# Sums of the up weights loaded straight into the operands' places, and more buffer places, in the feed-forward part of a two-stream trunk layer

## The chip, the cores and the metric

The kernel runs on one core of one Trainium2 chip. The metric is device time in microseconds (us) of one execution, the median of several. Five engines matter: TensorE (PE, its weight loads shown as PEld), VectorE (DVE), ScalarE (ACT), GpSimd (POOL) and SyncE (SP), which here issues every DMA.

## The reference

One layer (DEPTH is 1) over 2048 prompt positions and 32 sample positions, model width 1024, all in float32. A mixer (spatial gating and gated DeltaNet, with causal convolution) is followed by a feed-forward part with width 4096:

```python
h = rmsnorm(x, norm_mix_g[l]) * (1 + sc1) + sh1
m, nb, ns, vr = mixer(h, conv_state[l], delta_state[l], w_in[l], ...)
x = x + gt1 * m
h = rmsnorm(x, norm_ffn_g[l]) * (1 + sc2) + sh2
x = x + gt2 * (jnp.square(jax.nn.relu(h @ w_up[l])) @ w_down[l])
...
y = rmsnorm(x, final_norm_g)
```

The change touches the last two lines of the layer: `h @ w_up`, and what is queued around it.

## The kernel before

All work is first written down as operations of a `Program` (L201), with the engine, an estimated cost and the memory that each reads and writes. `schedule` (L237) then plays a list schedule: for each engine it keeps what is ready, ordered by priority and by the TensorE operation that comes due first, and it writes the program out in the order of the planned start times. So every engine, and SP's queue of DMAs, runs a fixed order; on the chip an instruction waits until what it needs is there, and everything behind it on its engine or queue waits too. Whatever changes an operation or a buffer changes the planned order everywhere.

Scratch memory is a set of `NSLOT` slots of 1056 floats per partition (25 of them). `ring` (L463) names places in slots that are used in turn: `new` takes the next place of a ring, and its next user has to wait until the last one is read.

**First half** (to about 1054 us of the profile): gates, projections, spatial gating and DeltaNet (`startup`, `mixers`), on matmuls into `g` banks, with many small matmuls into `L`, `C`, `B` and `M`. Its rings `pk1`, `pk2`, `kq1`, `kq2` and `E` hold tiles loaded for DeltaNet and for the norms.

**Feed-forward part** (`feed_forward`, L1512, from about 1054 us). The 2080 positions run in four blocks b = 0 to 3 of 520 positions, each as two groups of 260. A matmul in float32 is made of three fp32r matmuls: each operand x is split into a high part (ACT copies it to fp32r) and a low part (DVE or POOL subtracts the high part from x); `mm3` (L411) multiplies high by high, high by low and low by high.

The up product of one step s (16 steps of 256 hidden rows) takes a 2 x 2 block of weight pieces against a 2 x 2 block of h tiles and needs 7 products instead of 8, with four of its weight operands being sums of pieces. In block 0, `up_weights` (L1433) loads the four pieces, POOL makes the sums, they are split into high and low parts, and both parts are stored in DRAM tensors `su_d`. In blocks 1 to 3 the sums come back from `su_d`: each half (128x512, 256 KB) is loaded by a DMA into a place of the staging ring `uraw`, and ACT copies it from there into the operand's place (`wh` or `wl`). The three plain pieces are loaded from `w_u` into staging and split as before. The operands' places `uw` are 8 pairs (high, low) used in turn.

The down product has the same form (`ffn_down`, L1677): 16 half steps u, with sums of its weights kept in `sd_d`, loaded through the staging ring `draw` and split by ACT and DVE into `dw`. From the end of block 0 `uraw` and `draw` are one ring of 8 staging places. Up and down steps alternate on TensorE: down u of step q, then up 2q + 2 + u for the next step. `hidden` (L1629) forms relu squared and the sums of hidden tiles: DVE adds, ACT squares, POOL subtracts, ACT and DVE split.

At a change of block, `h2_values` (run from s = 8) has put the 28 combinations of h tiles of the next block into DRAM (`th_d`), and `h2_load` (L1411) loads them through the ring `fe` and splits them into the tiles `BH` and `BL`; these come free only as the last up step of the block is multiplied, so the loading falls beside the last down step. `settle`, `square` and `final` finish the block's result.

Lines that the profile names: L337 is every ACT instruction, L352 every tensor_tensor of DVE or POOL, L357 every scalar_tensor_tensor, L390 every DMA, L398 every matmul. Tiles in slots are named `s`, with a number in the order below; `f` is a PSUM bank of the feed-forward part. The DMA scratch of the program is left at its default.

Of the kernel before, what the change touches and what calls it, by code (L numbers as in the profile page):

```python
# [10 lines left out]
AF = mybir.ActivationFunctionType  # L11
# [5 lines left out]
P = 128  # L17
# [14 lines left out]
G = 260  # L32
# [3 lines left out]
NC_ = 17  # L36
SLOT = 1056
HALF = 528
NSLOT = 25

PE, DVE, ACT, POOL, DMA, NONE = range(6)
TABLES = {AF.Silu: "silu", AF.Gelu_apprx_tanh: "gelu", AF.Exp: "exp", AF.Ln: "ln"}
# [158 lines left out]
class Program:  # L201
# [35 lines left out]
    def schedule(self):  # L237

        ops = self.ops
        due = [i if o.eng == PE and o.prio == GEMM else len(ops) for i, o in enumerate(ops)]  # L240
        for i in reversed(range(len(ops))):
            due[i] = min([due[i]] + [due[j] for j in ops[i].succ])
        key = [(o.prio, due[i] if o.prio >= EVAC else i, i) for i, o in enumerate(ops)]
        free = [0.0] * 6
        port = [0.0] * 6
        wait = [[] for _ in range(6)]
        ready = [([], []) for _ in range(6)]
        table, grid = None, (P, P)
        order = []

        def release(i, t):
            o = ops[i]
            if o.eng == NONE:
                finish(i, t, t)
            else:
                heapq.heappush(wait[o.eng], (t, i))

        def finish(i, start, end):
            o = ops[i]
            o.start = start  # L260
            order.append((start, i))
            for j in o.succ:
                s = ops[j]
                s.ready = max(s.ready, end + o.lat + LATENCY.get((o.eng, s.eng), 0.0))
                s.npred -= 1
                if s.npred == 0:
                    release(j, s.ready)

        for i, o in enumerate(ops):
            if o.npred == 0 and o.start == 0.0 and o.eng != NONE:  # L270
                heapq.heappush(wait[o.eng], (0.0, i))
        for i, o in enumerate(ops):
            if o.npred == 0 and o.eng == NONE and not any(k == i for _, k in order[-1:]):
                finish(i, 0.0, 0.0)
                o.npred = -1

        other = {DVE: POOL, POOL: DVE}
        while True:
            best = None
            for e in range(5):  # L280
                shared = port[other[e]] - PORT if e in other else 0.0
                t = None
                if ready[e][0]:
                    t = free[e]
                elif ready[e][1]:
                    t = max(free[e], shared)
                if wait[e]:
                    at, i = wait[e][0]
                    at = max(free[e], at, shared if ops[i].port else 0.0)
                    t = at if t is None else min(t, at)  # L290
                if t is not None and (best is None or t < best[0]):
                    best = (t, e)
            if best is None:
                break
            t, e = best
            while wait[e] and wait[e][0][0] <= t:
                i = heapq.heappop(wait[e])[1]
                heapq.heappush(ready[e][ops[i].port], key[i])
            shared = port[other[e]] - PORT if e in other else 0.0
            tops = [q for q in (ready[e][0], ready[e][1] if shared <= t else None) if q]  # L300
            if not tops:
                continue
            i = heapq.heappop(min(tops, key=lambda q: q[0]))[-1]
            o = ops[i]
            end = t + o.cost
            if e == PE:
                if o.table and o.table != grid:
                    end += 195 if o.table == (P, P) else 135
                    grid = o.table
            elif o.table and o.table != table:  # L310
                end += 1280
                table = o.table
            free[e] = end
            if o.port:
                port[e] = end
            finish(i, t, end)
        assert len(order) == len(ops), (len(order), len(ops))
        self.span = max(free)
        order.sort()
        return [ops[i] for _, i in order]  # L320


class Kern:
# [211 lines left out]
    def setup(self):  # L535
# [14 lines left out]
        self.nslab, self.sn = 0, None  # L550
        self.slots = [{"m": Mem(SLOT), "t": None} for _ in range(NSLOT)]
        self.bmem = [Mem(512, whole=True) for _ in range(8)]
        self.banks = {"g": [0, 1, 2], "L": [3], "C": [4, 5], "B": [6], "M": [7]}
        self.rings, self.rshape = {}, {}
        for s in range(NSLOT):
            self.era(s, F32)
        rg = self.ring
        hv = lambda *ss: [(s, lo) for s in ss for lo in (0, HALF)]
        rg("pk2", [(0, 0), (1, 0)], (P, 4, 256))
        rg("kq2", hv(2), (P, 2, 256))  # L560
        rg("N", [(3, 288)], (P, 256))
        rg("U", [(3, 544)], (P, 256))
        self.z0 = self.slot(3, 0, (P, 9, 32))
        rg("nb", [(24, 0), (5, 0)], (P, SLOT))
        rg("pk1", [(6, 0)], (P, 3, 256))
        rg("kq1", hv(7), (P, 2, 256))
        rg("vt", [(8, 0), (8, 256)], (P, 256))
        rg("tmp", [(3, 800)], (P, 64))
        rg("jk", [(8, 768)], (P, 128))
# [36 lines left out]
            small(n, s, 17)  # L606
        rg("gt", [(17, pos[0] + 36 * e) for e in range(4)], (P, H, 9))
        rg("Q", hv(18, 19, 20), (P, 512))
        rg("E", hv(21, 22, 23), (P, 512))
        rg("va", [(q, 256 * e) for q in (18, 19, 20) for e in range(4)][:10], (P, 256))  # L610
        rg("raw", hv(18), (P, 516))
        rg("y", hv(19), (P, 512))
# [754 lines left out]

    def ffn_places(self):
        rg = self.ring
        e = [(s, G * e) for s in (6, 7, 16, 22, 23) for e in range(4)]  # L1370
        for tag, n in (("fe", 6), ("fs", 2), ("fx", 1), ("fp", 1), ("fu", 2), ("fv", 1), ("fr", 3), ("fk", 4)):
            rg(tag, e[:n], (P, G))
            e = e[n:]

# [58 lines left out]
    def up_weights(self, b, s):  # L1433

        quad = lambda q: self.i["w_u"][s, q]
        if b == 0:
            a11, a12, a21, a22 = (self.raw(self.uraw, quad(q)) for q in range(4))
            s1, s2 = (self.turn(self.uraw) for _ in range(2))
            self.tt(s1, a21, a22, ALU.add, POOL)
            self.tt(s2, s1, a11, ALU.subtract, POOL)  # L1440
        out = []

        def sum_(i, x):
            if b == 0:
                hl = self.operand(self.uw, x)
                for e in range(2):
                    self.dma(self.su_d[s][i][e], hl[e].f32())
            else:
                hl = self.turn(self.uw)
                for e in range(2):  # L1450
                    self.act(hl[e], self.raw(self.uraw, self.su_d[s][i][e]), AF.Copy)
            out.append(hl)

        plain = lambda q, x: out.append(self.operand(self.uw, x if b == 0 else self.raw(self.uraw, quad(q))))
        if b:
            s1 = s2 = s3 = s4 = a11 = a12 = a22 = None
        plain(0, a11)
        sum_(1, s2)
        sum_(0, s1)
        if b == 0:  # L1460
            s3 = self.turn(self.uraw) if len(self.uraw) > 6 else a11
            self.tt(s3, a11, a21, ALU.subtract, POOL)
        sum_(2, s3)
        if b == 0:
            s4 = s2
            self.tt(s4, a12, s2, ALU.subtract, POOL)
        sum_(3, s4)
        plain(1, a12)
        plain(3, a22)
        return out  # L1470
# [38 lines left out]
    def plain(self, b, q):  # L1509
        return b == 0 or (b, q) == (NB - 1, 7)  # L1510

    def feed_forward(self):  # L1512
# [8 lines left out]
        wv = [[view(k, e) for e in range(2)] for k in range(2)]  # L1521
        self.p.op(NONE, 0.0, fn, [v for w in wv for v in w], [])
        self.uw = [tuple(wv[k][e][:, 512 * j : 512 * j + 512] for e in range(2)) for k in (self.nslab % 2, (self.nslab + 1) % 2) for j in range(4)]
        for s in (3, 4, 5, 8, 9, 10, 11, 17, 18, 19, 20, 24):
            self.era(s, F32R)
        at = lambda n: slice(G * (n // 7), G * (n // 7) + G)
        self.hp = [[(self.BH[n % 7][:, at(n)], self.BL[n % 7][:, at(n)]) for n in range(4 * i, 4 * i + 4)] for i in range(7)]
# [4 lines left out]
        self.rp8, self.rpa, self.rpb = pairs[:16], pairs[10:], pairs[:10]  # L1532
        two = lambda s: [sl(s, 512 * e, (P, 512)) for e in range(2)]
        self.dw = [(x, y) for s, t in ((4, 5), (8, 9), (10, 3)) for x, y in zip(two(s), two(t))]
        self.uraw = two(0) + two(1) + two(2)
        self.draw = [self.raw1[0][:, 512 * e : 512 * e + 512] for e in range(2)] + two(21)
        self.acc = [[sl(12 + m // 2, G * (2 * (m % 2) + g), (P, G)) for g in range(2)] for m in range(KT)]
# [324 lines left out]
```

## Time and profile before

| what | value |
|---|---|
| median of 3 runs | 2437.33 us (2435.55 to 2437.97) |
| span of the profiled execution, first to last instruction (the page gives no other time of it) | 2450.8 us |
| mean granted TensorE clock | 0.989 |
| first feed-forward matmul starts, last one starts | 1054.1 us, 2439.6 us |
| DMA traffic of the whole program | 574.85 MB, mean 235 GB/s |

Busy time is what an engine spent in instructions; matmuls overlap, so TensorE's count of matmuls in a stage says more than its busy share. An idle time is put down to what released the engine last. In the rows of groups, busy time and mean length (ns) of one instruction are followed by the idle time before them.

### The profile page before, as it was taken

The page shows a single profiled execution, that of the slowest core. Times are in us where ns is not written, and L with a number is a line of the kernel's source. Part 1 is how long each engine was busy: PE and PEld are TensorE (multiplying, and loading weights), DVE is VectorE, ACT ScalarE, POOL GpSimd, SP SyncE. Part 2 cuts the span into 40 slices and gives each one's busy share as a digit, 9 for nine tenths or more (in the row PEclk, how much of TensorE's full clock was granted, in tenths as well). Part 3 has the DMA queues.
Part 4 walks back from the last instruction along what each step waited for, and adds up shares of the span by engine and source line. Part 5 has one row for each costly group of instructions (what it writes and reads, how often), then busy time and mean ns, then how long its engine had stood idle before and what let it go on. Part 6 is the DMA issues. An engine that isn't in the chain of part 4 may idle for free.

```text
span 2450.8 us, 53625 instructions
## 1 busy us (share of the span) xinstructions
PE 2372.3 (97%) x18786; PEld 2217.0 (90%) x18786; DVE 1749.2 (71%) x4041; ACT 1563.5 (64%) x3727; POOL 790.0 (32%) x1079
## 2 busy tenths in 40 slices
PE   7998999999999999999999999999899999899998
PEld 4876878999999878999999999999899999899998
DVE  5555666556665546488677778889788888877786
ACT  4454656455565435375455687777788877887774
POOL 2134422202432223455333453333721213511111
PEclk9999999999999899999999999999999999999999
DMA  8688667555457767888667787888788877787773
GB/s 305 206 298 264 211 199 243 143 180 161 145 181 215 239 183 231 269 273 275 240 215 244 251 265 242 268 273 275 240 266 289 267 256 231 248 279 220 246 232 117
DMA packets 389687, 574.85 MB, mean 235 GB/s; under 512 B 71628, under 2 KB 201568, under 8 KB 389416
## 3 DMA queue, kind: packets, MB, share of 16 engines
q1 hardware_dynamic: 389416, 571.42, 72.2%
q8 instruction: 148, 2.42, 0.4%
q14 instruction: 123, 1.01, 0.1%
HBM read 434.80 MB, written 136.45 MB: 233 GB/s over the span
## 4 chain that ended last, share of the span: by engine, by line
PE 27%; DVE 9%; DMA 8%; ACT 5%; issue 2%; POOL 1%; SPq 0%; DVEq 0%; ACTq 0%; POOLq 0%
PE f L398 27%; DVE s L352 6%; DMA s<-su_d 3%; ACT s L337 2%; DVE s L357 1%; ACT wh L337 1%; DMA s<-w_u 1%; DMA wr<-su_d 1%; DVE wl L352 1%; DVE BL L352 1%; ACT wl L337 1%; DMA wr<-w_u 1%; POOL s L352 1%; DMA s<-sd_d 1%; DMA s<-th_d 0%
## 5 line engine op out<-in xcount | busy, mean ns | idle before, releaser
L337 ACT ACTIVATE s<-s 128x260 f32<-128x260 f32 (+11 forms) x1398 | 611.5, 464 | 338.8 <-DVE s L357 99.5
L398 PE MATMUL f<-s,s 128*128 128x260 f32 x3984 | 538.5, 284 | 8.2 <-ACT s L337 3.6
L352 POOL TENSOR_TENSOR s<-s,s 128x260 f32<-128x260 f32 (+3 forms) x369 | 374.3, 1027 | 518.1 <-ACT s L337 377.0
L398 PE MATMUL f<-BH,wh 128*128 128x260 f32 x1800 | 514.0, 286 | 13.4 <-DVE s L352 9.1
L398 PE MATMUL f<-BH,wl 128*128 128x260 f32 x1800 | 511.1, 284 | 3.6 <-DVE wl L352 2.6
L398 PEld LDWEIGHTS f<-s,s 128*128 128x128 f32 x3984 | 501.8, 189 | 13.6 <-DVE s L352 6.3
L398 PE MATMUL f<-BL,wh 128*128 128x260 f32 x1800 | 509.9, 283 | 1.9 <-DVE BL L352 1.9
L352 DVE TENSOR_TENSOR s<-s,s 128x260 fp32r<-128x260 f32 (+5 forms) x740 | 413.4, 576 | 71.3 <-ACT s L337 43.6
L398 PE MATMUL g<-BH,wh 128*128 128x512 f32 (+2 forms) x1112 | 424.7, 382 | 0.0
L352 DVE TENSOR_TENSOR s<-f,s 128x260 f32<-128x260 f32 x856 | 345.6, 420 | 94.6 <-PE f L398 91.4
L398 PE MATMUL g<-BH,wl 128*128 128x512 f32 (+2 forms) x1112 | 395.0, 355 | 0.0
L398 PE MATMUL g<-BL,wh 128*128 128x512 f32 (+2 forms) x1112 | 393.8, 354 | 0.6 <-DVE BL L352 0.6
L398 PEld LDWEIGHTS f<-BH,wh 128*128 128x128 f32 x1800 | 340.4, 189 | 18.1 <-DVE s L352 6.7
L398 PEld LDWEIGHTS f<-BH,wl 128*128 128x128 f32 x1800 | 341.0, 189 | 5.1 <-DVE wl L352 3.7
L398 PEld LDWEIGHTS f<-BL,wh 128*128 128x128 f32 x1800 | 341.1, 190 | 2.8 <-DVE BL L352 2.7
L352 POOL TENSOR_TENSOR s<-s 128x260 f32<-128x260 f32 (+11 forms) x321 | 167.3, 521 | 531.8 <-DVE s L352 264.1
L337 ACT ACTIVATE wh<-s 128x512 fp32r<-128x512 f32 (+1 forms) x364 | 228.0, 630 | 83.8 <-DMA s<-w_u 25.2
L398 PE MATMUL f<-BH,s 128*128 128x260 f32 x1040 | 240.0, 285 | 0.9 <-ACT BH L337 0.6
L398 PEld LDWEIGHTS g<-BH,wh 128*128 128x128 f32 x1112 | 212.4, 191 | 24.7 <-issue 8.5
L398 PEld LDWEIGHTS g<-BH,wl 128*128 128x128 f32 x1112 | 211.9, 191 | 19.6
L398 PEld LDWEIGHTS g<-BL,wh 128*128 128x128 f32 x1112 | 213.2, 192 | 15.2 <-DVE BL L352 1.1
L357 DVE SCALAR_TENSOR_TENSOR s<-s,s,s 128x512 f32<-128x512 f32 (+6 forms) x318 | 165.0, 535 | 70.5 <-ACT s L337 40.5
(119 smaller groups left out, 3566.4 us busy)
## 6 DMA issues: line engine op xcount, KB each, us to landing
s<-su_d SPq DMA_DIRECT2D x288, 256.0 KB, 4.2
s<-w_u SPq DMA_DIRECT2D x168, 256.0 KB, 4.1
s<-w_d SPq DMA_DIRECT2D x150, 256.0 KB, 4.5
s<-sd_d SPq DMA_DIRECT2D x115, 256.0 KB, 4.0
wr<-su_d SPq DMA_DIRECT2D x96, 256.0 KB, 3.9
wr<-w_b SPq DMA_DIRECT2D x42, 512.0 KB, 5.6
wr<-w_d SPq DMA_DIRECT2D x68, 256.0 KB, 4.7
s<-x_d SPq DMA_DIRECT2D x128, 130.0 KB, 3.6
```

The costliest lines, as they stand in the source:

```text
L337: self.p.op(ACT, c, lambda: nc.scalar.activation(out=R(out), in_=R(in_), func=func, **{k: R(v) for k, v in kw.items()}), [out, accum], [in ...
L352: self.p.op(eng, c, lambda: e.tensor_tensor(out=R(out), in0=R(a), in1=R(b), op=op), [out], [a, b])
L357: self.p.op(DVE, c, lambda: nc.vector.scalar_tensor_tensor(out=R(out), in0=R(a), scalar=R(s), in1=R(b), op0=op0, op1=op1), [out], [a, s, b])
L398: nc.tensor.matmul(R(out), R(l), R(r), **kw)
```

## The change

1. `up_weights`: in blocks 1 to 3 the DMA loads each half of a sum straight into the operand's place; the staging place and ACT's copy fall away.
2. `dynamic_dma_scratch_size` is set to 1024 bytes, and three more slots (25, 26, 27) are taken from the memory set free: `NSLOT` 28.
3. The slots' use in the feed-forward part: `fe` gets 14 places instead of 6 (slots 25 and 26), and `uw` a ninth pair (slot 27).
4. Their use in the first half: `pk2`, `kq2` and `kq1` get a third place, `E` 8 places instead of 6.
5. `schedule`: bookkeeping of the operations that take no engine (a set `placed`), so that none is placed twice.

```diff
-NSLOT = 25
+NSLOT = 28
...
-        rg("pk2", [(0, 0), (1, 0)], (P, 4, 256))
-        rg("kq2", hv(2), (P, 2, 256))
+        rg("pk2", [(0, 0), (1, 0), (25, 0)], (P, 4, 256))
+        rg("kq2", hv(2) + [(26, 0)], (P, 2, 256))
...
-        rg("kq1", hv(7), (P, 2, 256))
+        rg("kq1", hv(7) + [(26, HALF)], (P, 2, 256))
...
-        rg("E", hv(21, 22, 23), (P, 512))
+        rg("E", hv(21, 22, 23, 27), (P, 512))
...
-        e = [(s, G * e) for s in (6, 7, 16, 22, 23) for e in range(4)]
-        for tag, n in (("fe", 6), ("fs", 2), ("fx", 1), ("fp", 1), ("fu", 2), ("fv", 1), ("fr", 3), ("fk", 4)):
+        e = [(s, G * e) for s in (6, 7, 25, 26, 16, 22, 23) for e in range(4)]
+        for tag, n in (("fe", 14), ("fs", 2), ("fx", 1), ("fp", 1), ("fu", 2), ("fv", 1), ("fr", 3), ("fk", 4)):
...
                 hl = self.turn(self.uw)
                 for e in range(2):
-                    self.act(hl[e], self.raw(self.uraw, self.su_d[s][i][e]), AF.Copy)
+                    self.dma(hl[e].f32(), self.su_d[s][i][e])
...
-        for s in (3, 4, 5, 8, 9, 10, 11, 17, 18, 19, 20, 24):
+        for s in (3, 4, 5, 8, 9, 10, 11, 17, 18, 19, 20, 24, 27):
             self.era(s, F32R)
...
+        self.uw.append(tuple(two(27)))
...
-    nc = bacc.Bacc("TRN2", target_bir_lowering=False, num_devices=1)
+    nc = bacc.Bacc("TRN2", target_bir_lowering=False, num_devices=1, dynamic_dma_scratch_size=1024)
```

What this does to the order shows best at two places. The first is SP's queue in block 3, where the sums of up step 8 are loaded (`su_d8_10` is sum 1 of step 8, high half; `s0`, `s1`, `s21` and `wr0` are staging places; `DMAHW` names a semaphore on which an earlier DMA reports that it has landed). Before:

```order
L390 DMA s21_426<-su_d8_10_279 128x512 [waits DMAHW1_49,DVE_49]
L390 DMA s21_426<-su_d8_11_280 128x512 [waits DMAHW2_49,DVE_49]
L390 DMA s1_406<-sd_d6_0_365 128x512 [waits DMAHW3_49,DMAHW0_49,Activation_49]
L390 DMA s0_405<-su_d8_00_277 128x512 [waits DMAHW6_49,DMAHW4_49,DVE_49]
L390 DMA s0_405<-su_d8_01_278 128x512 [waits DMAHW5_49,DVE_49]
L390 DMA wr0_96<-su_d8_31_284 128x512 [waits DMAHW7_49,DVE_49]
L390 DMA s1_406<-su_d8_21_282 128x512 [waits DVE_49]
L390 DMA s21_426<-w_u 128x512 [waits DMAHW1_49,Activation_49]
```

and with the change:

```order
L390 DMA wh_11751<-su_d8_10_279 128x512 [waits DMAHW1_49,PE_49]
L390 DMA wl_11752<-su_d8_11_280 128x512 [waits DMAHW2_49,PE_49]
L390 DMA s1_406<-sd_d6_0_365 128x512 [waits DMAHW3_49,DVE_49]
L390 DMA s21_426<-w_u 128x512 [waits DMAHW4_49,DVE_49]
L390 DMA s21_426<-w_u 128x512 [waits DMAHW5_49,DVE_49]
L390 DMA s0_405<-w_d 128x512 [waits DMAHW6_49,DVE_49]
L390 DMA s0_405<-sd_d7_2_371 128x512 [waits DMAHW7_49,DVE_49]
L390 DMA wh_11751<-su_d8_00_277 128x512 [waits DMAHW0_49,PE_49]
L390 DMA wl_11752<-su_d8_01_278 128x512 [waits DMAHW1_49,PE_49]
L390 DMA s27_10820<-su_d8_20_281 128x512 [waits DMAHW2_49,PE_49]
```

The loads of sums now go to `wh`, `wl` or slot 27 and wait for PE instead of for DVE or ACT; the loads of plain pieces and of down weights have moved ahead between them, since they alone use the staging places.

The second place is ACT's queue at the change from block 1 to 2, where the h tiles are copied into `BH` (`wl` and most `wh` rows copy sums; `s12` to `s15` are the block's result). Before:

```order
L337 ACTIVATE wh_11724<-wr0_96 128x512 [waits DMAHW0_49]
L337 ACTIVATE BH5_76<-s7_412 128x260 [waits DMAHW1_49]
L337 ACTIVATE s16_421<-s14_419 128x260 [waits Pool_49]
L337 ACTIVATE wl_11725<-s21_426 128x512 [waits DMAHW2_49]
L337 ACTIVATE BH0_71<-s6_411 128x260 [waits DMAHW3_49]
L337 ACTIVATE s16_421<-s14_419 128x260 [waits DVE_49,Pool_49]
L337 ACTIVATE wl_11725<-s0_405 128x512 [waits DMAHW4_49]
L337 ACTIVATE BH2_73<-s6_411 128x260 [waits DMAHW5_49]
L337 ACTIVATE wh_11726<-wr0_96 128x512 [waits DMAHW6_49]
```

and with the change:

```order
L337 ACTIVATE BH0_71<-s7_412 128x260 [waits DMAHW3_49]
L337 ACTIVATE BH0_71<-s26_431 128x260 [waits DMAHW4_49]
L337 ACTIVATE BH2_73<-s25_430 128x260 [waits DMAHW5_49]
L337 ACTIVATE s22_427<-s22_427 128x260 [waits DVE_49]
L337 ACTIVATE BH5_76<-s25_430 128x260 [waits DMAHW1_49]
L337 ACTIVATE s22_427<-s22_427 128x260 [waits Activation_49]
L337 ACTIVATE s4_1044<-s21_426 128x512 [waits PE_49]
L337 ACTIVATE s19_11747<-s22_427 128x260 [waits Activation_49]
L337 ACTIVATE s8_10671<-s0_405 128x512 [waits PE_49]
L337 ACTIVATE BH2_73<-s6_411 128x260 [waits DMAHW2_49]
```

No copies of sums stand between the `BH` rows any more; the tiles come from more places (`s25`, `s26`), and they stand further ahead, beside the hidden tiles of the block that ends.

More of the change, by code (lines that the diff above doesn't have):

```diff
@@ L248, in schedule @@
         table, grid = None, (P, P)
-        order = []
+        order, placed = [], set()
         def release(i, t):
@@ L260, in finish @@
             o.start = start
+            placed.add(i)
             order.append((start, i))
@@ L272, in schedule @@
         for i, o in enumerate(ops):
-            if o.npred == 0 and o.eng == NONE and not any(k == i for _, k in order[-1:]):
+            if o.npred == 0 and o.eng == NONE and i not in placed:
                 finish(i, 0.0, 0.0)
-                o.npred = -1
         other = {DVE: POOL, POOL: DVE}
```

## The prediction

> **What bounds the kernel now.** I read the busy totals first, then the busy time by stage, then the waits, then single instructions where the waits are longest.
>
> ```profile
> span 2450.8 us, 53625 instructions
> PE 2372.3 (97%) x18786; PEld 2217.0 (90%) x18786; DVE 1749.2 (71%) x4041; ACT 1563.5 (64%) x3727; POOL 790.0 (32%) x1079
> 0.00:1054.00 1054.00, 1015.75 (x7728) 879.75 (x7728) 616.65 (x1684) 552.97 (x1421) 322.66 (x613) 0.99 0.69 216
> 1300.00:1400.00 100.00, 100.00 (x837) 100.00 (x836) 77.60 (x151) 58.06 (x137) 37.16 (x31) 1.00 0.74 247
> 1400.00:1500.00 100.00, 98.46 (x810) 96.95 (x809) 80.50 (x157) 85.55 (x207) 54.56 (x57) 1.00 0.81 262
> 1500.00:1600.00 100.00, 96.77 (x802) 96.03 (x801) 86.07 (x184) 75.85 (x163) 29.54 (x29) 1.00 0.81 268
> 1600.00:1700.00 100.00, 98.59 (x809) 97.12 (x808) 88.90 (x192) 78.26 (x174) 34.13 (x35) 1.00 0.80 264
> 1700.00:1800.00 100.00, 91.64 (x693) 87.89 (x693) 82.55 (x166) 79.16 (x194) 56.95 (x62) 0.95 0.77 244
> 1800.00:1900.00 100.00, 98.97 (x819) 98.19 (x818) 85.44 (x186) 86.24 (x198) 20.01 (x24) 1.00 0.90 292
> 1900.00:2000.00 100.00, 99.14 (x820) 98.26 (x819) 81.77 (x188) 79.78 (x177) 19.77 (x24) 1.00 0.78 256
> 2000.00:2100.00 100.00, 97.90 (x797) 96.08 (x797) 88.96 (x192) 72.99 (x170) 32.22 (x37) 1.00 0.76 245
> 2100.00:2200.00 100.00, 92.67 (x735) 89.86 (x734) 78.28 (x158) 85.51 (x204) 31.86 (x38) 0.98 0.82 268
> 2200.00:2300.00 100.00, 99.34 (x816) 98.05 (x815) 78.07 (x175) 75.82 (x171) 17.48 (x22) 1.00 0.73 232
> 2300.00:2400.00 100.00, 100.00 (x837) 100.00 (x836) 87.69 (x211) 73.87 (x162) 13.59 (x17) 1.00 0.74 239
> ```
>
> Columns of a stage: its length, then busy time and count on PE, PEld, DVE, ACT and POOL, the granted TensorE clock, the DMA share, GB/s. TensorE bounds the kernel: 97% busy. The useful column is its count. Where nothing holds it, it issues 837 matmuls in 100 us, one every 0.1195 us (1300 to 1400, and again 2300 to 2400). So the most that any change beside TensorE can win in a stage is 837 minus its count, times 0.1195 us. The nine rows from 1400 to 2300 are short by 27, 35, 28, 144, 18, 17, 40, 102 and 21: 432 matmuls, 51.6 us. That is the pot. It lies in blocks 1 to 3 of the feed-forward part, where weight sums come back from DRAM. Two rows hold 246 of the 432 (29.4 us): the changes from block 1 to 2 (1700 to 1800) and from 2 to 3 (2100 to 2200).
>
> What holds TensorE there is in the waits of 1400 to 2300 (who waited for whom, total us, times, longest):
>
> ```profile
> PE f L398 <- DVE s L352: 11.7, 18, 2.0
> PE f L398 <- ACT BH L337: 3.7, 3, 1.7
> PE f L398 <- DVE BL L352: 3.5, 9, 1.2
> DVE BL L352 <- ACT BH L337: 35.4, 40, 3.5
> ACT wh L337 <- DMA s<-su_d: 20.3, 30, 2.2
> ```
>
> TensorE names DVE most, but DVE itself waited 35.4 us for ACT's BH tiles, and ACT had waited 20.3 us for sums to land in staging. ACT runs in order, so such a wait delays all behind it. The timeline of ACT and PE at a change of block shows it:
>
> ```profile
> 1753.05 0.63 ACT L337 ACTIVATE wh<-s 128x512 fp32r<-128x512 f32 x1 [0.98 <-DMA s<-su_d]
> 1754.44 0.63 ACT L337 ACTIVATE wh<-s 128x512 fp32r<-128x512 f32 x1 [0.44 <-DMA s<-su_d]
> 1755.55 0.41 ACT L337 ACTIVATE BH<-s 128x260 fp32r<-128x260 f32 x1
> 1756.01 0.39 PE L398 MATMUL f<-BH,wh 128*128 128x260 f32 x1 [1.70 <-ACT BH L337]
> ```
>
> TensorE stood 1.70 us for a BH tile; just ahead of that tile's copy ACT had stood 0.98 and 0.44 us for sums and copied them for 0.63 us each. Those are the copies that the change removes.
>
> **The change part by part.**
>
> *Removed: the copies.* Groups by form for `wl` (only sums reach `wl` through ACT), and the issues of the sums' loads:
>
> ```profile
> L337 ACT ACTIVATE wl<-s 128x512 fp32r<-128x512 f32 x144 | 89.6, 625 | 19.1 <-DMA s<-su_d 18.0 <-PE f L398 0.4
> L337 ACT ACTIVATE wl<-wr 128x512 fp32r<-128x512 f32 x48 | 30.0, 624 | 12.5 <-DMA wr<-su_d 12.3
> s<-su_d SPq DMA_DIRECT2D x288, 256.0 KB, 4.2
> wr<-su_d SPq DMA_DIRECT2D x96, 256.0 KB, 3.9
> ```
>
> 288 + 96 = 384 loads, one copy each; 192 are `wl`, 119.6 us; as many are `wh`, so ACT loses 239 us. Over the roughly 1050 us of blocks 1 to 3 that is 23 points: ACT falls from about 80% to about 57%, which is what it had from 1300 to 1400, where TensorE was full. DVE keeps its load. But from 2300 to 2400 TensorE was full with DVE at 87.7% and ACT at 73.9%, so a DVE near 88% does not by itself hold it. The copies are off TensorE, so their 239 us are worth only what ACT's lateness costs it, at most 51.6 us.
>
> For the two changes of block I take two thirds of 29.4 us: 19.6. There ACT is nearly solid, 28 h tiles must pass it while TensorE has only one down step left, and ACT also sits in front of DVE. The third that stays is DVE's and POOL's half of that work. For the other seven rows (186 matmuls, 22.2 us) I take 40%: 8.9. There the wait is mostly the chain from a hidden tile's sum over relu, square, high part (ACT) to the low part (DVE); ACT's queue is only one part of it. Sum: 28.5 us.
>
> *Moved: the loads.* Same 384 loads, same size, same queue; they now wait for TensorE to leave the place instead of for ACT to leave the staging tile. With nine places in turn instead of eight, I count in the change's order at least 97 matmuls between the last reader of a place and its next use, typically 181: 11.6 and 21.6 us at 0.1195 us. A load takes about 4.2 us, so it costs nothing while SP issues it within the other 7.4 us. What queues behind a load that waits on SP is the next `w_u`, `w_d` and `sd_d` loads. I take 0; the upper end is in the rivals. The staging ring of blocks 1 to 3 now carries 10 loads per pair of steps instead of 18, which can only help the rest.
>
> *Added: TensorE waits on a DMA's semaphore* where it waited on ACT's. Nearly every product already waits for one or two engines in the 1300 to 1400 row, and its 837 matmuls took no extra time; so 0, at most one lost issue (0.12 us) on each of 192 sums, 23 us.
>
> *Enlarged: the ring `fe` (6 to 14 places)* lets half of the 28 h tiles be loaded before the old ones are read; what it saves is part of the 19.6. *The rings of the first half* (`pk2`, `kq2`, `kq1`, `E`) rewrite the planned order before 1054 us. Its row shows TensorE 1015.75 us busy of 1054, so 38.3 us idle, much of it at the start, where no ring matters. The same chains are interleaved in nearly the same places; I take 0, with 6 us either way.
>
> *The smaller scratch.* All loads and stores of the program go through this one queue:
>
> ```profile
> q1 hardware_dynamic: 389416, 571.42, 72.2%
> ```
>
> No row shows anything that uses the scratch. I take 0; if landing doubled to 8.4 us, it would still be inside the 11.6.
>
> *Sum.* In the profiled execution 2450.8 - 28.5 = 2422.3 us of span. That page gives no time but its span, which is 13.5 us (0.6%) above the median of the timed runs, 2437.3; a difference carries over, so I take 2437.3 - 28.5 = **2409**.
>
> **Two rules weighed.** The low parts run on DVE and POOL; DVE rows, one POOL row at the same moment, and the whole group of 1400 to 2300:
>
> ```profile
> 1766.51 0.43 DVE L352 TENSOR_TENSOR BL<-s,BH 128x260 fp32r<-128x260 f32 x1 [0.81 <-ACT BH L337]
> 1772.16 2.08 DVE L352 TENSOR_TENSOR BL<-s,BH 128x260 fp32r<-128x260 f32 x1
> 1771.34 1.22 POOL L352 TENSOR_TENSOR rcol<-rcol,mhalf 128x2 f32<-128x2 f32 x2
> L352 DVE TENSOR_TENSOR BL<-s,BH 128x260 fp32r<-128x260 f32 x117 | 72.5, 641 | 35.9 <-ACT BH L337 35.4
> ```
>
> One instruction took 0.43 us alone and 2.08 us beside POOL; the mean of 117 is 0.641. The Trainium skill (SBUF — State Buffer, "Who interferes with whom") says that a DVE instruction with two SBUF inputs shares a port with a POOL instruction that reads SBUF, and that whichever comes second stands until the first is done. The trace agrees; by that rule, faster ACT copies only bring the same instructions to a port that is no wider, and the first rival below would be the outcome, 2427 instead of 2409.
>
> The granted clock is 0.95 in the row 1700 to 1800 and 0.98 in 2100 to 2200: 5 and 2 us lost, both inside the 29.4, though the longest wait of TensorE quoted above is 2.0 us. If these dips do not belong to the stalls, they stay, and two thirds of 7 us, 4.7, come off the sum: 23.8 us, 2414, inside the forecast's own bounds and with a part of its chance. The Trainium skill (TensorE: Matmul & The Clock Gate, "Why this matters for your kernels") warns only of idle gaps above about 3 us between bursts, so by that rule the stalls here did not cause the dips. I go by the rows: the clock was full in the stages without stalls.
>
> **The rivals.**
>
> *The low parts take ACT's place.* Of the 18.9 us of TensorE's waits quoted above, 15.2 are for DVE. If only ACT's own share goes (3.7 of 18.9, 20%), the pot gives 10 us: 2427. For: the 2.08 us row. Against: DVE's own 35.4 us of waiting for BH. 0.15.
>
> *SP is blocked (slower).* A load that waits for TensorE holds the queue, and the down weights behind it come late; TensorE then waits for them, releases places late, and the queue slips again.
>
> ```profile
> SPq L390 <- DVE s L352: 239.8, 279, 9.2
> ```
>
> SP's waits already reach 9.2 us (mean 0.86). It decides once a load is held longer than the 7.4 us of slack. At 0.9 us of lost TensorE time in each of 48 up steps (one SP wait of mean length) that is 43 us against 28.5 won: 2452. Against: that row is for DVE, and a typical place has 21.6 - 4.2 = 17.4 us. 0.08.
>
> *The late transfers pass to TensorE (no change).* The 20.3 us that ACT waited for `su_d` become TensorE's own; 8.2 of the 28.5 us are left, and 6 us lost in the first half leave 2.2: 2435. For: the DMA share is 0.73 to 0.90. Against: the same 11.6 us of lead. 0.07.
>
> **How the numbers follow.** The forecast, 2409, has 0.70. Its own bounds: all but a fifth of the pot plus 6 us in the first half gives 2390; the first rival with 5 us lost in the first half gives 2432. So 2390 to 2432 takes in the forecast and the first rival, and leaves out about 0.2. A measurement of this kernel tells about 0.2% (4.9 us) from no change: faster 0.70 + 0.15 = 0.85, same 0.07, slower 0.08.
>
> **What would show it.** Right: ACT's busy time falls by about 239 us, the copies into `wl` are gone, the two rows at changes of block rise from 693 and 735 to about 780 and 800 matmuls, DVE's wait for BH falls below 15 us, and everything before 1054 us ends within 6 us of where it did. The first rival: ACT falls as much, but the two rows stay below 760, with long BL instructions before them. SP blocked: waits of SP for PE above 7 us, and TensorE waiting for `w_d` or `sd_d`. Transfers: TensorE waiting for `su_d`. The forecast is wrong if TensorE's shortfall lies in rows that ACT's queue does not reach, or if the new order lengthens the first half.

## The result, and the profile after

| | before | after |
|---|---|---|
| median, us | 2437.65 (4 runs, 2435.55 to 2447.0) | 2402.39 (4 runs, 2401.22 to 2403.86) |
| ratio | 1 | 0.9857, 95% interval 0.983 to 0.9884 |
| span of the profiled execution | 2450.8 | 2400.6 |
| first, last feed-forward matmul starts | 1054.1, 2439.6 | 1040.5, 2389.3 |

The kernel is 35.3 us faster; 2409 was predicted, within 2390 to 2432. One execution of a kernel tried below, `fe six (3050)`, took 5823.84 us, more than twice any other; it is left out of that kernel's time and ratio. The profile of after: its page's totals, the stage up to 1040 us of the kernel before and then of the kernel after, and the nine stages (length, busy time and count on PE, PEld, DVE, ACT, POOL, clock, DMA share, GB/s).

```profile
0.00:1040.00 1040.00, 1001.75 (x7639) 866.29 (x7640) 608.49 (x1665) 544.00 (x1399) 316.91 (x606) 0.99 0.69 216
```

```profile
span 2400.6 us, 53253 instructions
PE 2341.2 (98%) x18786; PEld 2199.5 (92%) x18786; DVE 1757.9 (73%) x4041; ACT 1386.2 (58%) x3347; POOL 804.7 (34%) x1079
0.00:1040.00 1040.00, 1004.23 (x7727) 872.68 (x7727) 617.22 (x1689) 557.56 (x1429) 325.90 (x613) 1.00 0.70 220
1400.00:1500.00 100.00, 99.39 (x823) 98.45 (x822) 90.33 (x182) 73.49 (x177) 46.48 (x49) 1.00 0.88 290
1500.00:1600.00 100.00, 100.00 (x836) 100.00 (x836) 85.30 (x183) 57.05 (x130) 32.77 (x31) 1.00 0.79 264
1600.00:1700.00 100.00, 99.93 (x833) 99.68 (x832) 88.92 (x191) 59.33 (x138) 34.44 (x33) 1.00 0.80 273
1700.00:1800.00 100.00, 95.39 (x767) 92.31 (x766) 94.28 (x184) 77.86 (x197) 60.40 (x65) 1.00 0.85 279
1800.00:1900.00 100.00, 99.73 (x830) 99.32 (x830) 87.22 (x194) 60.11 (x137) 17.71 (x21) 1.00 0.86 291
1900.00:2000.00 100.00, 100.00 (x836) 100.00 (x836) 88.53 (x196) 57.83 (x132) 17.86 (x21) 1.00 0.77 254
2000.00:2100.00 100.00, 96.35 (x791) 94.82 (x790) 87.56 (x179) 69.50 (x175) 52.34 (x57) 1.00 0.81 261
2100.00:2200.00 100.00, 99.75 (x833) 99.54 (x832) 81.49 (x175) 59.45 (x135) 15.24 (x18) 1.00 0.75 249
2200.00:2300.00 100.00, 100.00 (x837) 100.00 (x836) 85.57 (x186) 58.36 (x133) 18.63 (x22) 1.00 0.70 232
```

The nine rows lack 14, 1, 4, 70, 7, 1, 46, 4 and 0 of 837 matmuls: 147 where before lacked 432. At 0.1195 us each, 285 matmuls or 34.1 us are recovered of a pot of 51.6. ACT is at 57 to 60% wherever no change of block lies, DVE did not move, and the granted clock is 1.00 in every row. What is left sits at the two changes of block: 1700 to 1800, and 2000 to 2100, into which the second one has moved.

The waits of 1400 to 2300 (who waited for whom, total us, times, longest), after:

```profile
PE f L398 <- DVE s L352: 5.4, 8, 1.4
PE f L398 <- DVE BL L352: 1.4, 2, 0.8
DVE BL L352 <- ACT BH L337: 2.5, 8, 0.9
ACT s L337 <- PE f L398: 108.2, 118, 3.8
ACT wh L337 <- PE f L398: 90.5, 28, 3.8
SPq L390 <- DVE s L352: 242.4, 206, 6.6
SPq L390 <- PE f L398: 98.7, 162, 1.7
```

DVE's wait for BH fell from 35.4 us to 2.5, TensorE's wait for DVE's `s` from 11.7 to 5.4, and TensorE no longer waits for ACT's BH (3.7 before). ACT now stands 198.7 us for TensorE: it has become early where it was late. SP does wait for TensorE, 162 times, but never longer than 1.7 us.

### The profile page after: what moved, and what is told of

Its sections match the earlier page's. It is cut to its first block, busy times and chain, and to the rows that moved or that the text cites. A ratio compares the mean times of both kernels' runs of the same rounds, so it can differ in the third digit from the quotient of the medians.

```text
span 2400.6 us, 53253 instructions
## 1 busy us (share of the span) xinstructions
PE 2341.2 (98%) x18786; PEld 2199.5 (92%) x18786; DVE 1757.9 (73%) x4041; ACT 1386.2 (58%) x3347; POOL 804.7 (34%) x1079
## 4 chain that ended last, share of the span: by engine, by line
PE 46%; DVE 4%; DMA 3%; issue 2%; ACT 2%; POOL 1%; SPq 1%; POOLq 0%; DVEq 0%; ACTq 0%
PE f L398 45%; DVE s L352 2%; POOL s L352 1%; ACT s L337 1%; DVE s L357 1%; DMA wr<-w_d 1%; SPq L390 1%; PE g L398 1%; DMA th_d<-s 0%; DMA s<-w_d 0%; DVE BL L352 0%; ACT wh L337 0%; DMA wr<-w_u 0%; DMA s<-th_d 0%; DMA s<-x_d 0%
## 5 line engine op out<-in xcount | busy, mean ns | idle before, releaser
L337 ACT ACTIVATE s<-s 128x260 f32<-128x260 f32 (+8 forms) x1421 | 633.6, 469 | 345.7 <-DVE s L352 101.3
L352 DVE TENSOR_TENSOR s<-s,s 128x260 fp32r<-128x260 f32 (+6 forms) x761 | 428.4, 579 | 76.6 <-ACT s L337 54.5
L398 PE MATMUL f<-BH,wh 128*128 128x260 f32 x1596 | 454.3, 285 | 8.8 <-DVE s L352 5.4
L398 PE MATMUL f<-BH,wl 128*128 128x260 f32 x1596 | 451.2, 283 | 1.1 <-DVE wl L352 1.1
L398 PE MATMUL f<-BL,wh 128*128 128x260 f32 x1596 | 449.9, 282 | 0.0
L398 PE MATMUL f<-BH,s 128*128 128x260 f32 x1448 | 318.2, 283 | 0.0
L398 PEld LDWEIGHTS f<-BH,wl 128*128 128x128 f32 x1596 | 300.6, 188 | 1.5 <-DVE wl L352 1.5
L398 PEld LDWEIGHTS f<-BL,wh 128*128 128x128 f32 x1596 | 300.9, 189 | 0.0
L398 PEld LDWEIGHTS f<-BH,s 128*128 128x128 f32 x1448 | 247.0, 188 | 0.2
L337 ACT ACTIVATE wh<-s 128x512 fp32r<-128x512 f32 (+1 forms) x197 | 124.4, 636 | 160.6 <-PE f L398 89.6
```

The source lines that it names most:

```text
L337: self.p.op(ACT, c, lambda: nc.scalar.activation(out=R(out), in_=R(in_), func=func, **{k: R(v) for k, v in kw.items()}), [out, accum], [in ...
L352: self.p.op(eng, c, lambda: e.tensor_tensor(out=R(out), in0=R(a), in1=R(b), op=op), [out], [a, b])
L398: nc.tensor.matmul(R(out), R(l), R(r), **kw)
```

## The experiments

**Theory:** ACT's copies of the sums, and ACT standing in order for them to land, held DVE and through it TensorE. **Rivals:** the added buffer places earn the gain; the rings of the first half earn 13 us of it (the feed-forward part began 13.6 us earlier in the profile of after); the gain is the luck of a new order. For each kernel the table gives the time and the ratio to the kernel before measured beside it. The other columns come from its one profile: the start of the first feed-forward matmul; the time from there to the start of the last one ("feed-forward"), which leaves out what happens ahead of the changed code; and from the nine rows from 1400 to 2300 the matmuls missing and the time lost to the clock, which is (1 - granted clock) x 100 us summed over the rows.

| kernel | us | ratio (95%) | starts | feed-forward, us | missing | clock, us |
|---|---|---|---|---|---|---|
| before | 2437.65 | 1 | 1054.1 | 1385.5 | 432 | 7 |
| before, again | 2436.25 (one run) | | 1042.2 | 1381.2 | 378 | 4 |
| after | 2402.39 | 0.9857 (0.983 to 0.9884) | 1040.5 | 1348.8 | 147 | 0 |
| direct loads only | 2418.43 | 0.993 (0.991 to 0.9951) | 1041.8 | 1361.6 | 233 | 3 |
| places only | 2432.05 | 0.9989 (0.9972 to 1.0005) | 1043.5 | 1374.7 | 356 | 7 |
| first-half rings as before | 2405.23 | 0.9873 (0.985 to 0.9896) | 1043.0 | 1349.8 | 145 | 0 |
| fe six | 2415.88 | 0.9916 (0.9895 to 0.9937) | 1040.6 | 1361.3 | 226 | 3 |
| no ninth pair | 2416.58 | 0.9919 (0.99 to 0.9939) | 1043.0 | 1357.9 | 218 | 7 |
| unused copies | 2423.20 | 0.9943 (0.9923 to 0.9963) | 1042.6 | 1367.8 | 289 | 5 |
| h tiles stored split | 2429.99 | 0.9976 (0.9963 to 0.9988) | 1050.9 | 1381.1 | 328 | 10 |
| after, other order (3050) | 2401.49 | 0.9864 (0.984 to 0.9888) | 1035.9 | 1350.9 | 152 | 0 |
| after, other order (2950) | 2413.34 | 0.991 (0.989 to 0.9929) | 1047.2 | 1352.8 | 173 | 2 |
| no ninth pair (3050) | 2407.32 | 0.9871 (0.9847 to 0.9895) | 1033.2 | 1350.3 | 175 | 0 |
| fe six (3050) | 2411.67 | 0.9901 (0.9878 to 0.9924) | 1038.8 | 1367.6 | 267 | 16 |

### The kernel before, again

No edit.

> The kernel before, unchanged, profiled once more. In its first profile the feed-forward part began at 1054.1 us, the changed kernel's at 1040.5, and its span was 2450.8 us, 13.5 above its median; its granted clock fell below 1 eight times before 1054 us, the changed kernel's only at 197, 494 and 1036. If the 13.6 us of the first half are a matter of that one execution (the clock), this profile starts the feed-forward part at about 1042 to 1046 us and has a span near 2438. If the larger rings of the first half earned them, it starts it at 1050 to 1055 again.

Measured: 2436.25 us, span 2434.5. Its stage up to 1040 us:

```profile
0.00:1040.00 1040.00, 1006.73 (x7711) 872.96 (x7712) 616.37 (x1683) 549.93 (x1417) 323.18 (x611) 0.99 0.69 218
```

It issues 7711 matmuls there, where the first profile of the same kernel has 7639 and the kernel after 7727. So 72 of the 88 matmuls that seemed won before 1040 us belonged to one execution; with a start at 1042.2 instead of 1054.1, 1.7 of the 13.6 us are left. The clock is a part of it only: stretches at half clock cost 13.7 us ahead of the feed-forward part in the first profile and 8.5 in this one (5.1 in the kernel after), 5.1 of the 11.9 us between the two; for the rest no cause is shown. The pot was also somewhat smaller in this execution: 378 matmuls, 45.2 us. Against it the kernel after recovers 231 matmuls, 27.6 us, instead of 34.1.

### Direct loads only

The kernel before with one line changed:

```diff
-                    self.act(hl[e], self.raw(self.uraw, self.su_d[s][i][e]), AF.Copy)
+                    self.dma(hl[e].f32(), self.su_d[s][i][e])
```

> The kernel before with only the first part of the change: the sums land in the operands' places, the copies go; 25 slots, the DMA scratch at its default, fe 6 places, uw 8 pairs. Theory (the copies and their place in ACT's order held TensorE): 2408 to 2416, about 25 us below the kernel before, ACT's busy time down by 170 to 240 us. Rival, places (fe and uw earn it): 2428 to 2434. Rival, first half: 13 us of the 35 come from the rings there, so about 2415 at best, with the feed-forward part starting where it did before. With one pair fewer, TensorE's places come free one turn later; if that matters, SP waits for PE over 3 us appear and the time stays above 2420.

Measured: 2418.43 us, 17 below the kernel before as measured beside it (2435.56), a little less than expected; half of the whole gain. DVE's wait for BH falls nearly as far as with the whole change, but TensorE still waits for BH itself (the waits of 1400 to 2300):

```profile
DVE BL L352 <- ACT BH L337: 8.1, 14, 1.6
PE f L398 <- ACT BH L337: 3.1, 3, 1.7
```

The stage of the first change of block:

```profile
1700.00:1800.00 100.00, 92.14 (x715) 89.18 (x714) 80.89 (x164) 69.70 (x177) 56.05 (x62) 0.97 0.83 261
```

Five of the other stages are filled (835, 831, 837, 836 and 837 matmuls from 1500, 1600, 1800, 1900 and 2200); the change of block is not: 715 against 767 with the whole change. SP waits for TensorE 1.9 us at the longest, so one pair fewer does not hold the queue.

### Places only

The changed kernel with that line turned back.

```diff
-                    self.dma(hl[e].f32(), self.su_d[s][i][e])
+                    self.act(hl[e], self.raw(self.uraw, self.su_d[s][i][e]), AF.Copy)
```

> The changed kernel with staging and ACT's copies of the sums put back; the larger rings, the ninth pair and the smaller scratch stay. Theory (copies): 2428 to 2437, ACT at about 64% again, the two rows at the changes of block still below 760 matmuls. Rival, places: 2405 to 2415. Rival, first half: about 2424, with the feed-forward part starting some 13 us earlier than in the kernel before and as long as before.

Measured: 2432.05 us, a ratio that cannot be told from 1. The waits of 1400 to 2300:

```profile
DVE BL L352 <- ACT BH L337: 26.1, 28, 2.4
ACT wh L337 <- DMA s<-su_d: 17.8, 27, 2.2
PE f L398 <- DVE s L352: 11.2, 12, 2.9
```

With ACT late, more places change little: it still stands 17.8 us for sums in this row, and DVE 26.1 us for ACT. The rival "places" falls in its plain form. One of the two rows at the changes of block (763) lies a little above the 760 expected, and the feed-forward part of this one profile is 6.5 and 10.8 us shorter than in the two profiles of the kernel before, so a small worth of the places alone is not ruled out.

### The first half's rings as before

The changed kernel with `pk2`, `kq2`, `kq1` and `E` as they were.

```diff
-        rg("E", hv(21, 22, 23, 27), (P, 512))
+        rg("E", hv(21, 22, 23), (P, 512))
```

(and the third places of the other three likewise.)

> The changed kernel with the rings of the first half (pk2, kq2, kq1, E) as they were. If those rings earn nothing (theory, and the clock as the cause of the shorter first half in the profile): 2400 to 2406, the feed-forward part starting within 3 us of 1040.5. If they earn the 13.6 us: 2413 to 2418, starting at 1052 to 1055.

Measured: 2405.23 us; its interval overlaps that of the whole change, and the feed-forward part starts at 1043.0. The rings earn nothing that this can tell.

### fe with six places

```diff
-        for tag, n in (("fe", 14), ("fs", 2), ...
+        for tag, n in (("fe", 6), ("fs", 2), ...
```

(the list of places without slots 25 and 26.)

> The changed kernel with fe at 6 places again (direct loads, ninth pair and first-half rings stay). Direct loads alone gave 0.993 of the time before, the whole change 0.986, so some 15 us come from places that pay only together with the direct loads. Theory (fe lets the h tiles of the next block in early): 2411 to 2417, the row 1700 to 1800 back from 767 matmuls to about 715, as with direct loads alone. Rival, the ninth pair: 2401 to 2406, that row still above 755.

Measured: 2415.88 us, 13.5 above the whole change. The waits of TensorE at the first change of block (1700 to 1750), with six places and then with fourteen:

```profile
PE f L398 <- ACT BH L337: 1.7, 2, 1.1
PE f L398 <- DVE BL L352: 1.4, 2, 1.0
```

```profile
PE f L398 <- DVE s L352: 1.6, 3, 0.7
PE f L398 <- DVE BL L352: 1.4, 2, 0.8
```

With fourteen places TensorE doesn't wait for a BH tile there, but its waits in these rows add up to about the same (3.1 and 3.0 us). The row 1700 to 1800 fell to 738, not quite to the 715 expected; the 29 matmuls lost, 3.5 us, are about what the clock took there (0.97, 3 us). The whole feed-forward part is 12.5 us longer.

### Eight pairs in uw

```diff
-        self.uw.append(tuple(two(27)))
```

> The changed kernel with eight pairs in uw instead of nine. Theory (fe is what pays): 2402 to 2407, the row 1700 to 1800 still above 755 matmuls. Rival, the ninth pair (with eight, loads wait longer for TensorE and hold the queue): 2411 to 2417, SP's longest wait for PE above 1.7 us and ACT again waiting long for DVE, as with direct loads alone (158 us against 38).

Measured: 2416.58 us, as the rival expects, and ACT waits long for DVE (163.5 us). But SP's longest wait for TensorE is 2.1 us (1.7 with nine pairs), too little to hold a queue, and the row 1700 to 1800 has 757, as the theory expects. Of the 71 matmuls that it lacks beyond the whole change, 46 are in one stage, 2000 to 2100 (745, clock 0.95). The timeline of DVE there:

```profile
2078.27 0.49 DVE L352 TENSOR_TENSOR s<-s,s 128x260 fp32r<-128x260 f32 x1 [1.29 <-ACT s L337]
2078.68 3.14 DVE L352 TENSOR_TENSOR s<-wr,s 128x512 fp32r<-128x512 f32 x1
2081.74 0.68 DVE L352 TENSOR_TENSOR s<-s,s 128x512 fp32r<-128x512 f32 x1
```

that of POOL at the same moment:

```profile
2079.14 1.43 POOL L352 TENSOR_TENSOR s<-s 128x260 f32<-128x260 f32 x2
2080.54 0.73 POOL L352 TENSOR_TENSOR s<-s,s 128x260 f32<-128x260 f32 x1
```

and the stages of 3.4 us that follow:

```profile
2082.20:2085.65 3.45, 1.60 (x12) 1.15 (x10) 3.17 (x9) 1.78 (x5) 3.08 (x2) 1.00 0.93 324
2085.65:2089.10 3.45, 2.79 (x12) 2.70 (x13) 0.00 (x0) 2.96 (x7) 3.45 (x6) 0.50 0.56 192
2089.10:2092.50 3.40, 2.88 (x14) 2.58 (x13) 2.92 (x6) 0.72 (x3) 1.55 (x3) 0.50 0.54 162
2092.50:2095.90 3.40, 3.40 (x18) 3.40 (x18) 1.21 (x4) 2.11 (x6) 1.44 (x2) 0.50 0.99 299
```

A subtraction of DVE that takes 0.68 us took 3.14 while POOL worked. Behind it stood DVE's part of the block's result (the small tile `rcol`, 2082.34); POOL waited 1.30 us for that and spent 3.21 us on its own two steps of `rcol`, and TensorE then stood 1.41 and 0.62 us for POOL's `rcol`. In this stretch TensorE is busy 1.60 of 3.45 us, and then it runs at half clock for three stretches. No pair of `uw` stands in this chain: DVE and POOL met there. So this run did not settle the ninth pair's part, and the order had to be varied by itself (below).

### The copies, unused

The changed kernel, and behind each direct load one ACT copy of the half into a tile `junk` that nobody reads:

```diff
                     self.dma(hl[e].f32(), self.su_d[s][i][e])
+                    self.act(self.junk, hl[e].f32(), AF.Copy)
```

> The changed kernel, and for each landed half of a sum one more ACT copy into a tile that nobody reads (384 copies; the outputs do not need them). ACT's load comes back without staging and without any copy ahead of the sum's use. Theory as predicted (ACT's load in its queue is what held DVE and TensorE): 2418 to 2430, ACT's busy time up by 200 to 240 us, DVE waiting above 20 us for BH again. Rival (the loss came from staging: sums landing late in places shared with plain pieces and down weights, and ACT standing for them): 2403 to 2411 although ACT is as busy as before.

Measured: 2423.20 us, 20.8 above the change and inside the theory's range. ACT's page total rises by 166.2 us to 1552.4, though the groups (1400 to 2300) show 623 ns for each copy:

```profile
L337 ACT ACTIVATE junk<-wh 128x512 f32<-128x512 f32 x154 | 96.0, 623 | 58.6 <-DMA wh<-su_d 58.2
```

ACT stands 58.2 us in this row (68.6 in all rows of `junk`) for sums to land although their users no longer need it; in the kernel before it was 50.0 in all (20.3, 12.4, 11.1 and 6.2). So load and standing come back together. A wait of 1400 to 2300:

```profile
DVE BL L352 <- ACT BH L337: 7.6, 17, 1.5
```

The path that was predicted for the copies' harm, DVE's wait for BH, stays small. The longest stall, in the timeline of PE, DVE and POOL:

```profile
1762.82 1.02 PE L398 MATMUL f<-s,s 128*128 128x260 f32 x3 [4.17 <-DVE s L352]
1755.61 6.22 DVE L352 TENSOR_TENSOR s<-s,s 128x260 fp32r<-128x260 f32 x2 [0.64 <-ACT s L337]
1756.03 4.90 POOL L352 TENSOR_TENSOR s<-s,s 128x260 f32<-128x260 f32 x7
```

TensorE stood 4.17 us for two instructions of DVE that took 6.22 us beside seven of POOL, and the row 1700 to 1800 lost 3 us more to the clock (0.97). So some 7 of the 20.8 us are that meeting. The feed-forward part is 1367.8 us, 15 to 19 more than the changed kernel takes for it in three orders (1348.8 to 1352.8, below); with the meeting taken off, 8 to 12 us are left that may be put down to the copies. The run does not part ACT's load from its standing.

### h tiles stored split

A candidate beyond the change: h tiles stored as high and low parts and loaded straight into `BH` and `BL`.

```diff
-                x = self.new("fe")
-                self.dma(x, self.th_d[b % 2][i][:, k])
-                self.split(*self.hp[i][k], x, POOL if b and k % 2 else DVE)
+                for j in range(2):
+                    self.dma(self.hp[i][k][j].f32(), self.th_d[b % 2][i][j][:, k])
```

> A candidate beyond the change: the combinations of h tiles are split when they are made and stored as high and low parts, so that at a change of block they are loaded straight into BH and BL (no ACT copy and no subtraction there; fe back to 6 places, its slots hold the split halves; twice the bytes for these tiles). The nine rows from 1400 to 2300 of the changed kernel still lack 166 matmuls, 19.8 us, 70 of them in the row 1700 to 1800 and 46 in 2000 to 2100. Theory (what is left at the turn is the split of h tiles): 2390 to 2400. Rival (what is left is the transfers, or the same work done a little earlier in the same queues): 2400 to 2412.

Measured: 2429.99 us, far worse than either expectation; the profiled execution was this kernel's slowest, 2444.83. (The nine rows of the changed kernel lack 147 matmuls, 17.6 us, not 166.) The stage of its change from block 0 to 1:

```profile
1400.00:1500.00 100.00, 92.33 (x731) 90.11 (x729) 71.90 (x141) 62.14 (x154) 43.73 (x48) 0.95 0.91 301
```

and a wait in it:

```profile
PE f L398 <- DMA wh<-su_d: 6.2, 2, 6.0
```

TensorE stood 6.0 us, to 1436.76, for a sum whose load was issued only at 1433.11: loads of h tiles stood in SP's queue up to 1423.8, and from 1426.78 eight stores of the block's result stood ahead of the sum. That the doubled h loads pushed it back is the likely reading; it is not shown. This is what the third rival of the prediction described, brought about by a different edit; one such wait doesn't account for all of the loss.

### The same kernels in another order

The planner's estimate of a DMA's latency, 3000 ns, is set to 3050 or 2950. Instructions, buffers and data stay the same; the order moves.

```diff
-DMA_LATENCY = 3000
+DMA_LATENCY = 3050
```

> The changed kernel with the planner's DMA latency at 3050 ns instead of 3000: same instructions, same buffers, another order here and there. It measures how much of any difference in this study is the luck of one order. If the places earn what they seemed to (the change 2402, without fe's places 2416, without the ninth pair 2417): 2398 to 2408. If the 2402 was a lucky order: 2410 to 2420, like its two reduced forms.

> The changed kernel with the planner's DMA latency at 2950 ns. As for 3050: 2398 to 2408 if the places earn it, 2410 to 2420 if the order did.

> Eight pairs in uw, planner's DMA latency 3050 ns. If the ninth pair earns its 14 us: 2411 to 2421 again, and in the feed-forward part at least three stretches of half clock, against none in the changed kernel's profile. If that was the order: 2400 to 2408, with at most one.

> fe at 6 places, planner's DMA latency 3050 ns. If fe's places earn their 14 us: 2410 to 2420 again, the row 1700 to 1800 below 750 matmuls. If that was the order: 2400 to 2408, the row above 755.

Measured: the changed kernel takes 2401.49 us in one order and 2413.34 in the other, one in each of the two ranges; so the luck of an order is worth up to 12 us of this kernel's time. Most of that lies ahead of the changed code: from the first to the last feed-forward matmul the three orders take 1348.8, 1350.9 and 1352.8 us, and the first one starts at 1040.5, 1035.9 and 1047.2. (The kernel before took 1385.5 and 1381.2 us for that part in its two profiles; it was tried in one order only.)

With `fe` at six, 2411.67: a loss of 13.5 us in one order and 10.2 in the other. By the time alone that is no more than what an order did. The row 1700 to 1800 doesn't tell either: it is below 750 in both (738 and 698), but the changed kernel has 735 there in the order of 2950. The feed-forward part does: 1361.3 and 1367.6 us with `fe` at six, 1348.8 to 1352.8 in the four profiles with fourteen places and nine pairs (the first-half rings put back among them). The longer one is of this kernel's slowest execution, 2420.12, but the shorter one is still 8.5 us beyond the four. So `fe`'s places earn something, given direct loads and nine pairs. With eight pairs 2407.32, ratio 0.9871 against 0.9864 with nine: not to be told apart here, and the clock is full, though the profiled execution was its fastest, 2396.68. Its feed-forward part is 1350.3 us, among those of nine pairs, where the first order had 1357.9. Together with the other order (0.9919 against 0.9857) the ninth pair's part stays open, between nothing and 14 us.

No kernel here beats the changed one by more than an interval.

## Why the prediction was right, point by point

- **The bound and the pot.** Right. TensorE bounds both kernels, and the gain is a recovery of its missing matmuls: 34.1 of 51.6 us by the nine rows (27.6 of 45.2 against the second profile of the kernel before), 35.3 by the medians. The feed-forward part alone shortened by 32 to 37 us (1348.8 against 1381.2 and 1385.5), and an order by itself moved that part by 4.0.
- **The two changes of block, 19.6 us.** Right in size, 20.6: the two rows lack 74 instead of 246. Not quite where it was expected: 767 and 833 against 780 and 800, since the second change has moved into the row before. With that row (2000 to 2100) counted in both times, the changes of block lack 120 instead of 286, 19.8 us.
- **The other seven rows, 8.9 us.** The term that was mis-sized. I took 40% of 186 matmuls, on the ground that most of the wait is the chain over hidden tiles; they lack 73 now, so 113 came back, 13.5 us (61%). Of those 73, 46 are the change of block that moved in; the other six rows went from 146 to 27. The chain is long, but ACT's lateness was most of what TensorE felt of it: with direct loads alone, five of these rows fill to 831 or more. Against the second profile of the kernel before, this term and the one above measure 10.5 and 17.1 us where 8.9 and 19.6 were forecast: one too small and one too large, so the nearness of their sum is in part luck.
- **ACT's 239 us.** Overstated: 177.3 by the page, 190.2 with direct loads alone. I multiplied 384 copies by the length of one, and back-to-back ACT instructions overlap (below); the whole change also has four more table loads on ACT (41 against 37, 5.1 us). What is left between these and 200 us stays open. The 20.3 us of standing for sums was one row of four, 50.0 in all, so the third rival, worked out from it, was priced too low too.
- **fe inside the 19.6.** Right in place and understated in weight. Direct loads alone gain 17 us; with nine pairs `fe`'s places are worth 10 to 13.5 more, and without direct loads all places together come to nothing that the time shows. The waits fit the reading that room is of no use while the engine that must empty it is late.
- **Moved loads and added waits, 0.** Right: SP's waits for TensorE end at 1.7 us, inside the 7.4 of slack, and TensorE never waits for a sum.
- **First half 0, with 6 us either way.** The rings' part right. By the first two profiles it looked 13.6 us wrong, and the second profile of the kernel before took 11.9 of that back. The other two orders of the changed kernel moved its end by 4.6 and 6.7 us, in one profile each.
- **Scratch 0.** Not tried by itself. The kernel with places only has the small scratch and the new bookkeeping of `schedule`, and takes 0.9989 of the time before.
- **Clock.** The forecast held that the dips belong to the stalls. They went with them: 7 us in the nine rows before (4 in its second profile), 0 after.
- **The rivals.** "SP is blocked" and "late transfers" did not happen. "The low parts take ACT's place" did not decide: TensorE's waits for DVE fell from 15.2 us to 6.8. But its mechanism is real: the low parts of `BL` did get longer, 711 ns against 641 (quoted for before), DVE's share in 1700 to 1800 rose to 94%, and where a meeting of DVE and POOL fell badly, it made the worst stalls of two experiments. The 0.43 us row that stood for an instruction alone was not alone: POOL worked on `rcol` from 1765.90 to 1767.34. So not every meeting lengthens an instruction.

```profile
L352 DVE TENSOR_TENSOR BL<-s,BH 128x260 fp32r<-128x260 f32 x116 | 79.8, 711 | 2.7 <-ACT BH L337 2.5
```

Two reasons remain argued, not shown: that ACT's load mattered more than its standing for sums; and that the harm went through DVE's wait for BH, which stayed small in the run that brought the copies back.

## What to carry to other kernels

Take the gain from the matmuls that are missing in a stage, not from the busy time that a change removes; an engine off the bound matters by what is late behind it. Buffer places paid here only once the engine that empties them was on time, so the two parts of such a change have to be tried together as well as alone. In a kernel whose order a planner sets, vary the order by itself before a difference of half a per cent is put down to an edit, and compare the length of the part that the edit touches, which the order moved by 4 us here, beside the whole time, which it moved by 12.

## What the runs showed of the hardware

**Short stalls can halve the clock.** The kernel before, stretches of 3.4 us around 1726 and 1753 us, then the kernel after around its deepest stall:

```profile
1722.70:1726.10 3.40, 3.40 (x31) 3.40 (x30) 1.63 (x4) 2.15 (x7) 2.99 (x3) 1.00 0.59 196
1726.10:1729.60 3.50, 1.72 (x13) 1.31 (x11) 3.30 (x6) 3.42 (x12) 3.50 (x5) 1.00 0.46 153
1729.60:1733.00 3.40, 3.20 (x14) 3.14 (x15) 3.40 (x5) 2.09 (x5) 3.40 (x4) 0.50 0.20 77
1753.40:1756.90 3.50, 1.39 (x10) 0.98 (x8) 1.58 (x3) 3.04 (x9) 1.47 (x2) 1.00 0.95 299
1756.90:1760.30 3.40, 3.40 (x15) 3.27 (x16) 1.44 (x4) 3.40 (x10) 1.50 (x2) 0.50 0.85 264
```

```profile
2056.40:2059.80 3.40, 3.40 (x30) 3.40 (x30) 2.10 (x6) 1.60 (x4) 2.34 (x3) 1.00 0.78 242
2059.80:2063.20 3.40, 2.04 (x17) 1.83 (x16) 2.81 (x6) 2.53 (x7) 2.33 (x3) 1.00 0.92 298
2063.20:2066.60 3.40, 2.83 (x24) 2.63 (x23) 3.40 (x6) 3.00 (x8) 2.07 (x3) 1.00 0.75 263
```

The third number is TensorE's busy time, behind it its matmuls. A stretch with 1.72 or 1.39 us of work is followed by one at half clock, which issues about 15 matmuls instead of 31 when full; one with 2.04 us is not. Between the first and last feed-forward matmul of the kernel before, the five stretches ahead of a dip were busy 1.39 to 2.02 us. The busy time of one stretch doesn't settle it: at 1552.1 us in the same profile 1.56 us were followed by full clock, and in `fe six (3050)` half clock followed stretches with 2.40 us (1749.2) and 2.46 (2087.1). So a stall that empties half a stretch is often paid a second time, with some 1.7 us (half of 3.4) for each stretch at half clock. The Trainium skill (TensorE: Matmul & The Clock Gate, "Why this matters for your kernels") warns of idle gaps above about 3 us; here the gaps in such a stretch came to 1.8 and 2.1 us in all, and the measurement decides.

**ACT instructions overlap.** Three copies of the kernel before, back to back:

```profile
1758.27 0.62 ACT L337 ACTIVATE wh<-s 128x512 fp32r<-128x512 f32 x1
1758.79 0.62 ACT L337 ACTIVATE wl<-s 128x512 fp32r<-128x512 f32 x1
1759.31 0.62 ACT L337 ACTIVATE wh<-s 128x512 fp32r<-128x512 f32 x1
```

Each is 0.62 us long and starts 0.52 after the one ahead; 384 x 0.52 = 200 us would have been the nearer figure for the copies. The Trainium skill (ScalarE: Activation LUTs, "What ACT_TABLE_LOAD costs") gives an overlap of about 93 ns for back-to-back instructions of this kind; the 0.10 us here agrees.

**A DVE instruction can be held through a whole run of POOL's.** The row of 6.22 us quoted from the run with the unused copies holds two: a 128x260 subtraction of 5.62 us, from 1755.61 to 1761.22, and a 128x512 one of 0.68, its usual length. The 128x260 form took 0.43 us at 1749.61 in the same profile. The long one ended 0.29 us behind the last of seven POOL instructions, each of about 0.72 us, that followed one another for 4.90 us; it stood for the whole run, not for the length of one of them.
